# Summing the last chunk's squares on TensorE, and reading a spread norm factor from PSUM, in a two-block transformer

## The chip, the cores and the metric

The kernel runs on one core of a Trainium2 chip. A core has TensorE (matmuls; PE in the profile, with PEld for its weight loads), VectorE (DVE), ScalarE (ACT), GpSimd (POOL) and SyncE (SP), which here does nothing but issue transfers. SBUF is the working memory, PSUM the accumulators of TensorE, in eight banks of 128 partitions x 512 fp32. The metric is the device time of one execution in microseconds (us), as the median of several. TensorE's clock has two levels, 1.2 and 2.4 GHz; the profile shows the granted share of the upper one.

## The reference

Input x is 512 tokens of 1024 features, fp32, one batch. The first block is two layers of mixing and MLP, each behind an RMS norm:

```
def rms_norm(x, g):
    y = x * lax.rsqrt(jnp.mean(x * x, axis=-1, keepdims=True) + NORM_EPS)
    return y * g
for l in range(2):
    proj = rms_norm(x, mix_norm_g[l]) @ w_in[l]
    ...                     # two attentions and a gated merge
    x = x + merged @ w_out[l]
    x = x + jnp.square(jax.nn.relu(rms_norm(x, mlp_norm_g[l]) @ w_up[l])) @ w_down[l]
```

The second block works on the result h, with shifts, scales and gates made from a vector c:

```
ada = jax.nn.silu(c) @ w_ada + b_ada        # 6 x 1024 values; w_ada has 6144 columns
shift1, scale1, gate1, shift2, scale2, gate2 = jnp.split(ada, 6, axis=-1)
hn = rms_norm(h, norm1_g) * (1.0 + scale1) + shift1
h = h + gate1 * (mamba_and_sparse_attention(hn) @ w_o)
hn2 = rms_norm(h, norm2_g) * (1.0 + scale2) + shift2
h = h + gate2 * mixture_of_experts(hn2)     # 32 experts of hidden size 256, two per token
out = rms_norm(h, final_g)
```

## The kernel before

Activations lie transposed: a feature chunk is a 128x512 tile (features on the partitions, tokens along), and x is eight such chunks. A product of fp32 precision is made of three fast passes: each operand is split into hi, rounded to the fast format (`hi_pool`, line 201, on GpSimd for weights; `hi_act`, line 204, on ScalarE), and lo = x - hi (`lo_dve`, line 207, on VectorE); TensorE then does hi.hi, lo.hi and hi.lo.

**Weights** come in 128x1024 tiles of 512 KB. `Weights.load` (line 87) has SyncE load tile i into a buffer of the tag `w_st`, which has three; hi and lo go to two buffers each (`w_hi`, `w_lo`), and a tile is asked for one unit ahead of its use. A unit is what TensorE does with one tile, 24 matmuls of 128x512 in the MLP. So w_hi of tile n+2 can be written only when TensorE is through with unit n.

**The six RMS factors.** A chunk that is complete is squared by ScalarE and added to `ssq` by VectorE (`square_chunk`, line 317; `sq` is the tile of squares). When the eighth is in, `norm_factor` sums over the partitions with four pairs of narrow fp32 matmuls against a column of ones (128x2, into the PSUM tag `s1`), VectorE adds the epsilon (`r_v`, line 327) and GpSimd takes the power (`r_tm`, line 225). `norm_finish` spreads the factor: VectorE writes four diagonal tiles (line 341), TensorE multiplies them by ones into one PSUM bank of the tag `s1`, which has one buffer, and ScalarE copies that to SBUF (`r_bc`, line 344). It is done ahead of each layer's attention (24 and 756 us into the span), ahead of each MLP (405 and 1135 us), ahead of the second block (1493 us) and, through `norm_factor` alone, ahead of the experts (2427 us).

**`Block2.norm`** (1489 to 1511 us) multiplies the eight chunks by the spread factor (line 908: chunks 0, 2, 4, 6 on VectorE, 1, 3, 5 on GpSimd; line 906: chunk 7 on VectorE), adds the shift into hi on ScalarE, and makes lo on VectorE (line 910). TensorE's first unit of the second block waits for these.

**`ada_tile`** (line 875) computes the second block's shifts and gates beside the second layer's MLP, one tile of w_ada per weight unit in the 16 units before 1220 us: SyncE loads 512 KB (line 878), VectorE multiplies by silu(c) with a running sum (line 879). Its tile `wada` is of the same tag `w_st` as the weights: weight tiles and ada tiles take turns in three buffers. Weight tile n is `w_stn` in the orders below; units 166 to 181 are in this stretch.

**What sets the order.** The order of each engine's instructions, and which of a tag's buffers a tile gets, are chosen by a scheduler at build time, with a simulated timeline of the whole program. An edit in one place can so move instructions far from it.

Of the kernel before, what the change touches and what calls it, by code (L numbers as in the profile page):

```python
# [15 lines left out]
OP = mybir.AluOpType  # L16
# [3 lines left out]
P = 128  # L20
# [3 lines left out]
KC = 8  # L24
# [110 lines left out]
class K:  # L135
# [173 lines left out]
    def square_chunk(self, c, x):  # L309
        nc = self.nc  # L310
        sq = self.t([P, T], "sq", bufs=2)
        self.act(sq, x, AF.Square)
        if c == 0:
            self.ssq = self.t([P, T], "ssq")
            nc.vector.tensor_copy(self.ssq, sq)
        else:
            nc.vector.tensor_tensor(self.ssq, self.ssq, sq, op=OP.add)

    def norm_factor(self):

        nc = self.nc
        ps = self.bank("s1", 1, (P, 8))
        for tb in range(4):
            self.mm(ps[:, 2 * tb:2 * tb + 2], self.ssq[:, tb * P:(tb + 1) * P], self.ones[:, 0:2],
                    tb == 0, tb == 3, True)
        v = self.t([P, 4], "r_v")
        nc.vector.tensor_scalar(v, ps.rearrange("p (a b) -> p a b", b=2)[:, :, 0], 1.0 / D, EPS,
                                op0=OP.mult, op1=OP.add)
        r = self.t([P, 4], "r_tm", bufs=2)
        self.rsqrt(r, v)  # L330
        return r

    def norm_finish(self):

        nc = self.nc
        r = self.norm_factor()
        dg = self.t([P, T], "sq", bufs=2)
        pb = self.bank("s1", 1)
        for tb in range(4):
            c = slice(tb * P, (tb + 1) * P)  # L340
            nc.vector.tensor_scalar(dg[:, c], self.ident, r[:, tb:tb + 1], None, op0=OP.mult)
            self.mm(pb[:, c], self.ones, dg[:, c], tb == 0, tb == 3, True)
        rb = self.t([P, T], "r_bc")
        self.nc.scalar.copy(rb, pb)
        return r, rb

    def o_halves(self, dst, ps_lo, ps_hi, shape):
# [499 lines left out]
class Block2:  # L847
# [48 lines left out]
    def norm(self, x, rb, hi, lo):  # L896

        k, nc = self.k, self.k.nc
        for c in range(KC):
            s = slice(c * T, (c + 1) * T)  # L900
            shift = self.ada[:, c:c + 1]
            xc = x[c]
            if c == KC - 1:

                xc = k.t([P, T], "of", bufs=2)
                nc.vector.scalar_tensor_tensor(xc, x[c], self.mod[:, 0, c:c + 1], rb, op0=OP.mult, op1=OP.mult)
            else:
                (nc.gpsimd if c in (1, 3, 5) else nc.vector).tensor_tensor(xc, xc, rb, op=OP.mult)
            k.act(hi[:, s], xc, AF.Identity, bias=shift)
            nc.vector.scalar_tensor_tensor(lo[:, s], xc, shift, hi[:, s].bitcast(F32), op0=OP.add, op1=OP.subtract)  # L910

# [1407 lines left out]
```

## Time and profile before

| what | before |
|---|---|
| median of 3 runs | 2802.71 us (2795.55 to 2803.74) |
| profiled execution | 2804.59 us, its span 2802.5 us, granted clock 0.985 |
| TensorE (PE) busy | 2680.8 us, 96% of the span |
| VectorE (DVE) busy | 1805.6 us, 64% |
| ScalarE (ACT) busy | 982.8 us, 35% |
| GpSimd (POOL) busy | 1114.4 us, 40% |

The profile is of one execution. In a timeline a row gives the start, the time from the first start to the last end of the instructions it holds (xN), engine, line, operation, output and inputs, and in brackets how long the engine sat idle before it and what ended that. A busy TensorE is not one at its peak: at the lower clock the same matmuls take longer.

### The profile page before, as it was taken

The numbers are of one execution on the slowest core, as the hardware profiler recorded it, in microseconds if no ns is written. First come the engines' busy times: TensorE is split into PE (matmuls) and PEld (weight loads), VectorE is DVE, ScalarE is ACT, GpSimd is POOL, SyncE is SP. The second block draws the span as 40 slices with busy tenths as digits, with TensorE's granted clock in tenths as the row PEclk, the third lists the DMA queues.
The fourth block names the chain that finished last, engine by engine and source line by source line (L and its number), as shares of the span: only waits on it lengthen the run. The fifth ranks groups of instructions, "written<-read, shape, count | busy, mean of one in ns | idle before, by whom it ended". The sixth has DMA issues, their size and how long they took to land.

```text
span 2802.5 us, 36356 instructions
## 1 busy us (share of the span) xinstructions
PE 2680.8 (96%) x13308; PEld 2179.6 (78%) x13308; DVE 1805.6 (64%) x2984; ACT 982.8 (35%) x1836; POOL 1114.4 (40%) x1539
## 2 busy tenths in 40 slices
PE   7999999999989999999998999999999999799996
PEld 6788888888878878787887988776877887677774
DVE  6866553334476656555745767576777776598887
ACT  3433322011134451210212245455334233277773
POOL 4544244143264533332423445445666565201102
PEclk9999999999999999999999999999999999899998
DMA  4111232223312123456634331132212225369986
GB/s 141 53 61 47 97 120 98 98 98 107 111 62 67 38 77 134 158 180 187 193 124 148 112 118 35 53 113 78 74 64 72 68 84 199 123 239 335 357 319 229
DMA packets 112522, 355.46 MB, mean 127 GB/s; under 512 B 19559, under 2 KB 24551, under 8 KB 111696
## 3 DMA queue, kind: packets, MB, share of 16 engines
q1 hardware_dynamic: 104480, 340.61, 35.9%
q10 hardware_dynamic: 5264, 6.29, 0.6%
q0 software_dynamic: 2592, 6.15, 0.6%
q8 instruction: 107, 1.75, 0.3%
q14 instruction: 79, 0.65, 0.1%
HBM read 329.51 MB, written 27.26 MB: 127 GB/s over the span
## 4 chain that ended last, share of the span: by engine, by line
PE 75%; DVE 8%; POOL 5%; DMA 5%; issue 4%; ACT 2%; SPq 0%; POOLq 0%; DVEq 0%; ACTq 0%
PE ps_d L179 43%; PE ps_w L179 8%; PE ps_o L179 5%; PE ps_b L179 4%; PE ps_gu L179 4%; DMA wada<-in_w_ada_t 4%; PE ps_po L179 3%; PE ps_tr L179 2%; DVE w_lo L207 2%; PE ps_e L179 2%; PE ps_tr L1525 1%; PE ps_s L179 1%; POOL w_hi L201 1%; POOL W L493 1%; POOL S L1165 1%
## 5 line engine op out<-in xcount | busy, mean ns | idle before, releaser
L179 PE MATMUL ps_d<-S,w_hi 128*128 128x512 f32 x4448 | 1413.6, 395 | 20.4 <-POOL c_vec L195 7.3
L179 PEld LDWEIGHTS ps_d<-S,w_hi 128*128 128x128 f32 x4448 | 828.6, 189 | 197.8 <-POOL c_vec L195 14.5
L179 PE MATMUL ps_d<-S,w_lo 128*128 128x512 f32 x2224 | 873.3, 394 | 18.5 <-DVE w_lo L207 18.1
L201 POOL TENSOR_SCALAR w_hi<-w_st 128x1024 fp32r<-128x1024 f32 x332 | 373.6, 1125 | 731.1 <-PE ps_d L179 603.0
L207 DVE TENSOR_TENSOR w_lo<-w_st,w_hi 128x1024 fp32r<-128x1024 f32 x343 | 448.2, 1307 | 292.9 <-POOL w_hi L201 267.2
L179 PEld LDWEIGHTS ps_d<-S,w_lo 128*128 128x128 f32 x2224 | 419.2, 188 | 111.8 <-DVE w_lo L207 28.2
L217 ACT ACTIVATE f<-ps_d 128x512 f32<-128x512 f32 x64 | 38.3, 598 | 455.8 <-PE ps_d L179 455.8
L2055 POOL DMA_INDIRECT moe_rows<-my,idx x14 | 32.7, 2335 | 266.1 <-DVE my L2049 138.9
L879 DVE SCALAR_TENSOR_TENSOR W<-wada,W 128x1024 f32<-128x1024 f32 x48 | 69.6, 1449 | 97.3 <-DMA wada<-in_w_ada_t 97.3
L201 POOL TENSOR_SCALAR S<-of 128x512 fp32r<-128x512 f32 x96 | 105.3, 1097 | 67.3 <-DVE of L744 31.2
L195 POOL MEMSET c_vec<- 1x1 f32 x424 | 35.8, 89 | 238.5 <-PE ps_d L179 201.4
L1516 POOL TENSOR_SCALAR pw<-pw,ri,gn 128x128 f32<-128x128 f32 (+3 forms) x128 | 90.4, 713 | 53.9 <-DVE ri L1515 45.8
L207 DVE TENSOR_TENSOR m_lo<-S,m_hi 128x1024 fp32r<-128x1024 f32 x81 | 98.5, 1222 | 17.5 <-ACT m_hi L204 16.2
L207 DVE TENSOR_TENSOR S<-of,S 128x512 fp32r<-128x512 f32 x96 | 80.0, 833 | 33.0 <-POOL S L201 31.0
L204 ACT CAST m_hi<-S 128x1024 fp32r<-128x1024 f32 x81 | 84.5, 1049 | 29.0 <-PE ps_gu L179 13.9
L179 PE MATMUL ps_w<-w_hi,S 128*128 128x512 f32 x256 | 83.1, 403 | 9.6 <-POOL w_hi L201 9.6
L217 ACT ACTIVATE pw<-pw,mx 128x128 f32<-128x128 f32 (+3 forms) x128 | 71.4, 559 | 30.2 <-DVE mx L1513 29.5
L179 PE MATMUL ps_w<-S,w_hi 128*128 128x512 f32 x256 | 79.1, 389 | 0.0
L179 PEld LDWEIGHTS ps_tr<-gS,S 128*128 128x128 f32 x512 | 70.7, 196 | 8.7 <-issue 2.2
L179 PE MATMUL ps_tr<-gS,S 128*128 128x256 f32 x512 | 75.4, 293 | 1.1 <-DVE gS L1950 1.1
L207 DVE TENSOR_TENSOR w_lo<-S,w_hi 128x1024 fp32r<-128x1024 f32 x53 | 64.6, 1222 | 10.8 <-ACT w_hi L204 9.8
L796 DVE TENSOR_TENSOR f<-ps_d,r_sq 128x512 f32<-128x512 f32 x32 | 22.1, 690 | 73.2 <-PE ps_d L179 73.2
(576 smaller groups left out, 4815.9 us busy)
## 6 DMA issues: line engine op xcount, KB each, us to landing
w_st<-in_w SPq DMA_DIRECT2D x374, 512.0 KB, 3.3
S<-in_w SPq DMA_DIRECT2D x158, 512.0 KB, 5.6
wada<-in_w_ada_t SPq DMA_DIRECT2D x48, 512.0 KB, 3.6
x<-S SPq DMA_DIRECT2D x16, 256.0 KB, 2.0
moe_rows<-S ACTq DMA_DIRECT2D x1, 4096.0 KB, 15.7
ssm_away<-nf SPq DMA_DIRECT2D x12, 256.0 KB, 2.0
S<-in_x_t SPq DMA_DIRECT2D x8, 256.0 KB, 6.8
S<-in_x_t SPq DMA_DIRECT2D x1, 2048.0 KB, 7.6
```

The source lines that it names most:

```text
L179: return self.nc.tensor.matmul(out, l, r, start=start, stop=stop, skip_group_check=sk)
L195: b = self.nc.gpsimd.memset(self.beat_at[:, i:i + 1], 0.0)
L201: self.nc.gpsimd.tensor_scalar(hi, x, 1.0, 1.0, op0=OP.mult, op1=OP.mult)
L204: self.last_hi = self.nc.scalar.copy(hi, x)
L207: return self.nc.vector.tensor_tensor(lo, x, hi.bitcast(F32), op=OP.subtract)
L217: i = self.nc.scalar.activation(out, x, f, bias=bias, scale=scale, **kw)
L493: nc.gpsimd.tensor_scalar(p[h][:, 256 - nk:], p[h][:, 256 - nk:], ri[:, h:h + 1], 1.0, op0=OP.mult, op1=OP.mult)
L879: nc.vector.scalar_tensor_tensor(junk, w, 1.0, self.cs, op0=OP.mult, op1=OP.mult, accum_out=self.ada[:, j:j + 1])
L1165: nc.gpsimd.tensor_tensor(y, y, rb, op=OP.mult)
L1516: nc.gpsimd.tensor_scalar(w, w, ri[:, c], gate[:, c], op0=OP.mult, op1=OP.mult)
L1525: nc.tensor.transpose(pt[:, h], p[:, h, j * P:(j + 1) * P], k.ident)
L2055: self.k.nc.gpsimd.indirect_dma_start(out=self.Y, out_offset=bass.IndirectOffsetOnAxis(ap=self.idx[:, j:j + 1], axis=0), in_=y, in_offset= ...
```

## The change

`square_chunk` no longer adds the eighth chunk's squares; it keeps them in `self.sq`, and `norm_factor` sums `ssq` and `sq` with eight pairs of narrow matmuls that accumulate in the same PSUM tile, in place of four. `norm_finish` keeps its PSUM tile as `self.pb`; in `Block2.norm`, VectorE multiplies chunks 0, 1, 3, 5 and 7 by that PSUM tile, and GpSimd chunks 2, 4 and 6 by the copy in SBUF.

```diff
--- before.py
+++ after.py
@@ -313,6 +313,8 @@
         if c == 0:
             self.ssq = self.t([P, T], "ssq")
             nc.vector.tensor_copy(self.ssq, sq)
+        elif c == KC - 1:
+            self.sq = sq
         else:
             nc.vector.tensor_tensor(self.ssq, self.ssq, sq, op=OP.add)
 
@@ -320,9 +322,10 @@
 
         nc = self.nc
         ps = self.bank("s1", 1, (P, 8))
-        for tb in range(4):
-            self.mm(ps[:, 2 * tb:2 * tb + 2], self.ssq[:, tb * P:(tb + 1) * P], self.ones[:, 0:2],
-                    tb == 0, tb == 3, True)
+        for i, x in enumerate((self.ssq, self.sq)):
+            for tb in range(4):
+                self.mm(ps[:, 2 * tb:2 * tb + 2], x[:, tb * P:(tb + 1) * P], self.ones[:, 0:2],
+                        i + tb == 0, i == 1 and tb == 3, True)
         v = self.t([P, 4], "r_v")
         nc.vector.tensor_scalar(v, ps.rearrange("p (a b) -> p a b", b=2)[:, :, 0], 1.0 / D, EPS,
                                 op0=OP.mult, op1=OP.add)
@@ -342,6 +345,7 @@
             self.mm(pb[:, c], self.ones, dg[:, c], tb == 0, tb == 3, True)
         rb = self.t([P, T], "r_bc")
         self.nc.scalar.copy(rb, pb)
+        self.pb = pb
         return r, rb
 
     def o_halves(self, dst, ps_lo, ps_hi, shape):
@@ -903,9 +907,11 @@
             if c == KC - 1:
 
                 xc = k.t([P, T], "of", bufs=2)
-                nc.vector.scalar_tensor_tensor(xc, x[c], self.mod[:, 0, c:c + 1], rb, op0=OP.mult, op1=OP.mult)
+                nc.vector.scalar_tensor_tensor(xc, x[c], self.mod[:, 0, c:c + 1], k.pb, op0=OP.mult, op1=OP.mult)
+            elif c in (2, 4, 6):
+                nc.gpsimd.tensor_tensor(xc, xc, rb, op=OP.mult)
             else:
-                (nc.gpsimd if c in (1, 3, 5) else nc.vector).tensor_tensor(xc, xc, rb, op=OP.mult)
+                nc.vector.tensor_tensor(xc, xc, k.pb, op=OP.mult)
             k.act(hi[:, s], xc, AF.Identity, bias=shift)
             nc.vector.scalar_tensor_tensor(lo[:, s], xc, shift, hi[:, s].bitcast(F32), op0=OP.add, op1=OP.subtract)
 
```

VectorE has 6 instructions fewer, TensorE 24 pairs more; SyncE's order is the same. Lines from 315 on move down by 2 to 6 (line 908 becomes 912 and 914, line 879 becomes 883).

In `Block2.norm`, VectorE's rows before, from the last weight split to the first line-910 rows, with the semaphores they wait for:

```order
L207 TENSOR_TENSOR w_lo229_11621<-w_st229_11618,w_hi229_11620 128x1024 [waits DMAHW1_49,Pool_49]
L317 TENSOR_TENSOR ssq_1123_11066<-ssq_1123_11066,sq_1144_11548 128x512 [waits Activation_49]
L327 TENSOR_SCALAR r_v_1146_11556<-ps_s1_1145_11551 128x4 [waits PE_49]
L341 TENSOR_SCALAR sq_1148_11560<-c_ff_6_88,r_tm_1147_11558 128x128 [waits Pool_49]
L341 TENSOR_SCALAR sq_1148_11560<-c_ff_6_88,r_tm_1147_11558 128x128 x3
L908 TENSOR_TENSOR S2_913_8803<-S2_913_8803,r_bc_1150_11570 128x512 [waits Activation_49]
L908 TENSOR_TENSOR S2_913_8803<-S2_913_8803,r_bc_1150_11570 128x512 x3
L906 SCALAR_TENSOR_TENSOR of_1153_11595<-S2_913_8803,c_mod_1119_10996,r_bc_1150_11570 128x512 [waits DVE_49]
```

The same place with the change:

```order
L207 TENSOR_TENSOR w_lo229_11636<-w_st229_11633,w_hi229_11635 128x1024 [waits DMAHW1_49,Pool_49]
L330 TENSOR_SCALAR r_v_1146_11571<-ps_s1_1145_11562 128x4 [waits PE_49]
L344 TENSOR_SCALAR sq_1148_11575<-c_ff_6_88,r_tm_1147_11573 128x128 [waits Pool_49]
L344 TENSOR_SCALAR sq_1148_11575<-c_ff_6_88,r_tm_1147_11573 128x128 x3
L914 TENSOR_TENSOR S2_913_8812<-S2_913_8812,ps_s1_1149_11576 128x512 [waits Activation_49]
L914 TENSOR_TENSOR S2_913_8812<-S2_913_8812,ps_s1_1149_11576 128x512 x3
L910 SCALAR_TENSOR_TENSOR of_1153_11610<-S2_913_8812,c_mod_1119_11008,ps_s1_1149_11576 128x512 [waits DVE_49]
```

The last addition to ssq is gone from VectorE's row, and the first multiplication, which now reads PSUM (`ps_s1`), waits for a semaphore of ScalarE as it did before.

GpSimd's rows there before and with the change, in which only the chunks differ:

```order
L201 TENSOR_SCALAR w_hi229_11620<-w_st229_11618 128x1024 [waits DMAHW1_49,DVE_49,PE_49]
L225 TENSOR_TENSOR r_tm_1147_11558<-r_v_1146_11556,c_vec_7_90 128x4 [waits DVE_49]
L908 TENSOR_TENSOR S2_913_8803<-S2_913_8803,r_bc_1150_11570 128x512 [waits Activation_49]
L908 TENSOR_TENSOR S2_913_8803<-S2_913_8803,r_bc_1150_11570 128x512 x2
L201 TENSOR_SCALAR w_hi230_11673<-w_st230_11671 128x1024 [waits DMAHW3_49,PE_49,Pool_49]
```

```order
L201 TENSOR_SCALAR w_hi229_11635<-w_st229_11633 128x1024 [waits DMAHW1_49,DVE_49,PE_49]
L225 TENSOR_TENSOR r_tm_1147_11573<-r_v_1146_11571,c_vec_7_90 128x4 [waits DVE_49]
L912 TENSOR_TENSOR S2_913_8812<-S2_913_8812,r_bc_1150_11585 128x512 [waits Activation_49]
L912 TENSOR_TENSOR S2_913_8812<-S2_913_8812,r_bc_1150_11585 128x512 x2
L201 TENSOR_SCALAR w_hi230_11688<-w_st230_11686 128x1024 [waits DMAHW3_49,PE_49,Pool_49]
```

Its three multiplications stay, with the same wait.

In the ada stretch, VectorE's rows before, from the ada tile after weight tile 172 on:

```order
L879 SCALAR_TENSOR_TENSOR W4_912_8802,c_ada_904_8771<-wada_993_9547,W4_905_8772 128x1024
L207 TENSOR_TENSOR w_lo173_9474<-w_st173_9471,w_hi173_9473 128x1024
L207 TENSOR_TENSOR S4_945_9125<-of_984_9463,S3_942_9122 128x512
L207 TENSOR_TENSOR w_lo174_9514<-w_st174_9511,w_hi174_9513 128x1024
L879 SCALAR_TENSOR_TENSOR W4_912_8802,c_ada_904_8771<-wada_997_9587,W4_905_8772 128x1024
L207 TENSOR_TENSOR S6_946_9126<-of_988_9503,S5_943_9123 128x512
L207 TENSOR_TENSOR w_lo175_9554<-w_st175_9551,w_hi175_9553 128x1024
L879 SCALAR_TENSOR_TENSOR W4_912_8802,c_ada_904_8771<-wada_1001_9627,W4_905_8772 128x1024
L207 TENSOR_TENSOR S6_946_9126<-of_992_9543,S5_943_9123 128x512
L207 TENSOR_TENSOR w_lo176_9594<-w_st176_9591,w_hi176_9593 128x1024
L879 SCALAR_TENSOR_TENSOR W4_912_8802,c_ada_904_8771<-wada_1005_9667,W4_905_8772 128x1024
L207 TENSOR_TENSOR S6_946_9126<-of_996_9583,S5_943_9123 128x512
```

The same place with the change:

```order
L883 SCALAR_TENSOR_TENSOR W4_912_8811,c_ada_904_8780<-wada_993_9559,W4_905_8781 128x1024
L207 TENSOR_TENSOR w_lo173_9486<-w_st173_9483,w_hi173_9485 128x1024
L207 TENSOR_TENSOR S4_945_9133<-of_984_9475,S3_942_9130 128x512
L883 SCALAR_TENSOR_TENSOR W4_912_8811,c_ada_904_8780<-wada_997_9599,W4_905_8781 128x1024
L207 TENSOR_TENSOR w_lo174_9526<-w_st174_9523,w_hi174_9525 128x1024
L207 TENSOR_TENSOR S6_946_9134<-of_988_9515,S5_943_9131 128x512
L883 SCALAR_TENSOR_TENSOR W4_912_8811,c_ada_904_8780<-wada_1001_9639,W4_905_8781 128x1024
L207 TENSOR_TENSOR w_lo175_9566<-w_st175_9563,w_hi175_9565 128x1024
L207 TENSOR_TENSOR S6_946_9134<-of_992_9555,S5_943_9131 128x512
L883 SCALAR_TENSOR_TENSOR W4_912_8811,c_ada_904_8780<-wada_1005_9679,W4_905_8781 128x1024
L207 TENSOR_TENSOR w_lo176_9606<-w_st176_9603,w_hi176_9605 128x1024
L207 TENSOR_TENSOR S6_946_9134<-of_996_9595,S5_943_9131 128x512
```

Before, w_lo174 stands ahead of the ada tile wada_997, and so it goes on. With the change w_lo174 to w_lo178 stand behind the ada tile that precedes them. The buffers move too: with the change each of wada_973, 977, 981 and so on to 1013 (eleven tiles) is loaded into the buffer of the weight tile whose w_lo stands just ahead of it in VectorE's order (wada_973 in that of w_st167, wada_1013 in that of w_st177); before, that holds for five tiles, wada_981 to wada_997. w_lo166 and w_lo167 are parted too: with the change the ada tile wada_969 stands between them.

## Rows read from the trace of the kernel before

**Rows 1.** Windows: busy us of each engine, granted clock, DMA share, GB/s.
```profile
400.00:420.00 20.00, 20.00 (x98) 16.81 (x97) 8.67 (x13) 5.52 (x9) 9.86 (x9) 1.00 0.25 81
740.00:770.00 30.00, 30.00 (x148) 25.36 (x147) 10.65 (x13) 1.73 (x3) 7.50 (x8) 1.00 0.30 97
1489.40:1512.60 23.20, 13.38 (x47) 9.21 (x47) 16.36 (x26) 7.20 (x11) 8.26 (x6) 0.71 0.50 190
2500.00:2750.00 250.00, 243.85 (x1180) 186.11 (x1179) 214.27 (x323) 177.66 (x284) 32.69 (x14) 0.99 0.93 337
```

**Rows 2.** Timeline of 1489 to 1499 us, up to the spread factor.
```profile
1491.15 0.63 ACT L217 ACTIVATE sq<-S 128x512 f32<-128x512 f32 x1 [8.06 <-DVE S L797]
1492.18 0.68 DVE L317 TENSOR_TENSOR ssq<-ssq,sq 128x512 f32<-128x512 f32 x1
1493.00 1.02 PE L179 MATMUL ps_s<-c_ff,ssq 128*128 128x2 f32 x8 [3.55 <-DVE ssq L317]
1497.89 0.59 ACT L344 COPY r_bc<-ps_s 128x512 f32<-128x512 f32 x1 [6.11 <-PE ps_s L179]
```

**Rows 3.** Timeline of 1499 to 1516 us, the multiplications and behind.
```profile
1498.51 5.74 DVE L908 TENSOR_TENSOR S<-S,r_bc 128x512 f32<-128x512 f32 x4 [2.26 <-ACT r_bc L344]
1498.55 5.14 POOL L908 TENSOR_TENSOR S<-S,r_bc 128x512 f32<-128x512 f32 x3 [3.21 <-ACT r_bc L344]
1500.10 0.76 PE L179 MATMUL ps_b<-S,w_hi 128*128 128x512 f32 x1 [2.25 <-ACT S L217]
...
1504.83 4.05 DVE L910 SCALAR_TENSOR_TENSOR S<-S,c_ada,S 128x512 fp32r<-128x512 f32 x6
1510.26 0.98 PE L179 MATMUL ps_b<-S,w_hi 128*128 128x512 f32 x3 [0.53 <-DVE S L910]
```

**Rows 4.** Instructions of line 908: ns min/median/max.
```profile
L908 DVE TENSOR_TENSOR S<-S,r_bc x4: 693/1759/1765, 1498.5 to 1502.5; 128x512 f32<-128x512 f32 x4
```

**Rows 5.** Instructions of line 678, which multiply a PSUM tile.
```profile
L678 DVE TENSOR_TENSOR S<-ps_d,r_bc x16: 677/692/694, 98.6 to 978.2; 128x512 f32<-128x512 f32 x16
```

**Rows 6.** GpSimd's groups by shape: busy us, mean ns, idle before.
```profile
L1496 POOL TENSOR_TENSOR S<-nsa_c,rk 128x512 f32<-128x512 f32 x2 | 2.1, 1043 | 2.0 <-DVE rk L1491 2.0
```

**Rows 7.** Timeline at 405 us, the MLP norm's sums amid matmuls.
```profile
405.32 0.39 PE L179 MATMUL ps_d<-S,w_hi 128*128 128x512 f32 x1
406.36 0.49 PE L179 MATMUL ps_d<-S,w_hi 128*128 128x512 f32 x1
```

**Rows 8.** Timeline at 1139 us, the second MLP's first weights.
```profile
1139.27 0.80 PE L179 MATMUL ps_d<-S,w_lo 128*128 128x512 f32 x1 [2.80 <-DVE w_lo L207]
```

**Rows 9.** Timeline at 26 us.
```profile
26.74 0.79 PE L179 MATMUL ps_w<-w_lo,S 128*128 128x512 f32 x1 [1.52 <-DVE w_lo L207]
```

**Rows 10.** Timeline at 2426 us.
```profile
2426.23 0.66 PE L1717 MATMUL ps_e<-c_ff,S 128*128 128x128 f32 x4 [0.62 <-DVE S L1709]
```

**Rows 11.** Timeline of 1154 to 1163 us: one round of the ada stretch.
```profile
1155.61 1.21 DVE L207 TENSOR_TENSOR w_lo<-w_st,w_hi 128x1024 fp32r<-128x1024 f32 x1
1156.86 0.33 SPq L878 DMA_DIRECT2D wada<-in_w_ada_t  x1
1161.31 1.23 DVE L879 SCALAR_TENSOR_TENSOR W<-wada,W 128x1024 f32<-128x1024 f32 x1 [3.88 <-DMA wada<-in_w_ada_t]
```

**Rows 12.** VectorE's timeline of 1129 to 1225 us.
```profile
1143.10 1.23 DVE L879 SCALAR_TENSOR_TENSOR W<-wada,W 128x1024 f32<-128x1024 f32 x1 [0.28 <-DMA wada<-in_w_ada_t]
1181.46 1.23 DVE L879 SCALAR_TENSOR_TENSOR W<-wada,W 128x1024 f32<-128x1024 f32 x1 [2.86 <-DMA wada<-in_w_ada_t]
```

**Rows 13.** GpSimd's timeline of 1136 to 1220 us.
```profile
1211.26 1.06 POOL L201 TENSOR_SCALAR w_hi<-w_st 128x1024 fp32r<-128x1024 f32 x1 [2.64 <-PE ps_d L179]
...
1216.70 1.06 POOL L201 TENSOR_SCALAR w_hi<-w_st 128x1024 fp32r<-128x1024 f32 x1 [2.64 <-PE ps_d L179]
```

**Rows 14.** Timeline of 2771 to 2776 us, the last experts.
```profile
2771.82 3.37 DVE L2154 TENSOR_TENSOR S<-S,my 128x1024 f32<-128x1024 f32 x1
2775.39 1.22 PE L179 MATMUL ps_po<-m_hi,mhs 128*128 128x512 f32 x2 [4.26 <-DVE mhs L207]
```

## The prediction

> **What bounds the kernel now.** I read the busy shares first: TensorE is at work for 96% of the span (the table). So I went by windows, to see where it isn't. In the layers it is busy for all of a stretch (20.00 of 20 us, 30.00 of 30); around the second block's norm it is busy for 13.38 of 23.2 us, at a mean granted clock of 0.71; among the experts it is at 244 of 250 us while the transfers take 0.93 of the DMA engines [rows 1]. Time saved on another engine counts only where TensorE waits for it. Then I read the timelines of the six norms and, with the order of instructions beside them, of the stretches in which instructions moved.
>
> **Second block's norm (the part that both edits meet).** The eighth chunk's squares are ready at 1491.15 + 0.63 = 1491.78; the addition (0.68) follows, and TensorE starts its sums at 1493.00 [rows 2]. With the change the sum of `ssq` can be done before, and that of `sq` starts some 0.1 us behind ScalarE, at 1491.9: 1.1 us gained, with four pairs behind it as before. All that follows up to the copy, which ends at 1497.89 + 0.59 = 1498.48 [rows 2], comes 1.1 sooner, at 1497.4. VectorE's multiplications don't start before that copy ends: their first instruction waits for ScalarE in the order with the change. Reading PSUM therefore doesn't take the copy off the path; without that wait they would start 0.6 us sooner.
>
> The Trainium skill (PSUM — Partial Sum Buffer, section "PSUM bank collisions raise a hardware error") says that two engines must not touch the same bank and quadrant at one time, two readers included, and that the back end therefore adds a dependency between them. By that rule the wait is forced, as ScalarE's copy and VectorE's multiplication read one bank; the order with the change agrees, and no run so far shows what it costs. By the rule the sum stays as it is worked out below; were readers free of one another, it would be 0.6 us less.
>
> What reading PSUM can change is how long the multiplications take. Before, VectorE's four take 5.74 us while GpSimd's three take 5.14 [rows 3], and one of the four took 693 ns while the median is 1759 [rows 4]: the two engines take turns. Multiplications that read one operand from PSUM take 692 ns in 16 cases [rows 5], and GpSimd, with the same shape from SBUF, 1043 ns on average [rows 6]. I take 0.69 and 1.04, since the rows before show VectorE slow only in the company of GpSimd with both operands in SBUF; at the other end they stay at 1.76. VectorE then needs 4 x 0.69, 0.69 for chunk 7 and 8 x 0.675 for the lo's (4.05 for six [rows 3]), in all 8.9 us: its last lo is done at 1506.3, and TensorE, which ends 1.0 us behind its last wait for a lo [rows 3], at 1507.3. By TensorE itself: its unit is 24 matmuls, which take 5.44 us at the upper clock (5.44 us from unit to unit among the layers [rows 13], 0.227 each) and twice that, 10.9, at the lower, which is half of it; from a first hi 1.1 us sooner than 1500.10 [rows 3] it would end at 1509.9 if the clock never rose. The clock of 0.71 in the stretch says that it does rise on the way. Before, the unit ended at 1510.26 + 0.98 = 1511.24. Between 1507.3 and 1509.9 I take 1508.6: **-2.6 us**; the ends are -1.1 (the multiplications stay slow) and -4.0.
>
> **The sums in the middle of matmuls.** Four pairs of narrow sums at 405 us part two matmuls by 406.36 - 405.32 = 1.04 us [rows 7], where they would be 0.23 apart: 0.81 us. TensorE is full there and at 756 us [rows 1], so four pairs more cost 2 x 0.81 = **+1.6 us** (0 to 2.9, the upper end for pairs that are strewn among matmuls). VectorE's additions that go were hidden there: nothing comes back. At 1135 us TensorE waits 2.80 us for VectorE's w_lo right behind [rows 8], and the extra pairs go into that wait: 0, and 0.81 without it. At 26 us TensorE waits 1.52 us for a w_lo [rows 9] that stands behind the last addition on VectorE: **-1.0** (-1.5 to 0). At 2426 us the pairs partly fill a wait of 0.62 [rows 10]: **+0.4** (0 to 1).
>
> **The ada stretch (1135 to 1220 us), a side effect.** Here the order moves. Before, five ada tiles are loaded into the buffer of the weight tile whose w_lo stands just ahead of them on VectorE. Each round is a ring that nothing overlaps: w_lo at 1155.61 to 1156.8, issue at 1156.86, multiplication at 1161.31 when the tile is in [rows 11], and then the next w_lo. From the multiplication at 1161.31 three rounds lead to that at 1181.46: 6.72 us each [rows 11, 12]. TensorE needs 1216.70 - 1211.26 = 5.44 us for a unit [rows 13]. So such a round holds it back by 1.28 us when no lead is left. After five, w_lo174 stands ahead of the ada tile and the ring is broken.
>
> With the change there are eleven rounds in a row. The multiplication of wada_969, at 1143.10 [rows 12] in both orders, ends at 1144.3, w_lo167 behind it at 1145.4, and w_lo178 eleven rounds of 6.72 later, at 1219.3. Unit 178 needs it from its second matmul on, so it ends near 1219.3 + 23 x 0.227 = 1224.5. Before, unit 178 ended at 1216.70, when its buffer went to w_hi of tile 180 [rows 13]. The difference is **+7.8 us**; nothing behind gives it back, since TensorE bounds the units that follow. The ends are 0 (the ring isn't the limit, or transfers land sooner) and +11 (rounds of 7). SyncE's order is the same, and behind each waiting ada issue on its queue stands the next weight load, which is 2 rounds ahead of its use.
>
> **Experts and tail.** Many rows of the experts are interleaved anew, with equal work. In the tail an addition of line 2154 (3.37 us) stands on VectorE just ahead of the lo on which TensorE waits 4.26 us [rows 14]; with the change it stands five rows sooner, but GpSimd's four additions, which slow VectorE there, end when they did. I take **0** (-4 to +5).
>
> **Sum.** -2.6 + 1.6 - 1.0 + 0.4 + 7.8 + 0 = +6.2 us on the profiled execution of 2804.59. That one is 1.9 above the median of 2802.71; the forecast for the median is 2802.71 + 6.2 = 2808.9, say 2809, 0.22% slower.
>
> **Rivals.**
> - *The ring does not hold TensorE back.* The five rounds before cost less than 5 x 1.28 in all if a lead was there, and a transfer may land sooner. Then the rest is left: 6.2 - 7.8 = -1.6, 2801. Against it: eleven rounds use up any lead that five did not.
> - *The experts are worse interleaved.* There the DMA engines are at 0.93 [rows 1], and one weight tile is 512 KB; at 337 GB/s that is 1.6 us by itself. Where a weight load's issue moves behind a use, one load is bare; with three or more such places beyond the ring, 5 us come on top: 2814. For it: the rows there are shuffled widely. Against it: SyncE's order, by which the loads go out, is the same. It decides from a third such place on.
> - *The kernel gets faster.* The norm gains its 4.0, the sums hide altogether, the ring costs nothing and the experts gain 4: -4.0 - 1.5 - 4 = -9.5 with the gain of 1.5 at 26 us, 2793. It needs all of these at once; the wait on ScalarE's copy already takes a part of what the edit could give.
> - *The change does not do what it says*: VectorE reads PSUM but stays at 1.76 us a multiplication. Only 1.1 of the 2.6 is left and the sum is +7.7: 2810. This lies in the forecast's own range.
>
> **How the numbers follow.** What a measurement of this kernel can tell from no change is about 0.3%, 8.4 us: below 2794.3 is faster, above 2811.1 slower. The forecast with its own range of 2805 to 2815 has 0.61 (0.38 of it within the bound, 0.23 above), no ring 0.15 (within), worse experts 0.16 (above), faster 0.08 (0.07 below the bound). That makes 0.07 faster, 0.54 the same, 0.39 slower. The range of 2800 to 2818 leaves out the faster case, a part of no ring and the top of worse experts.
>
> **What would show it.** In the profile after: TensorE's sums of `sq` at 0.1 us behind ScalarE's last square and the first unit of the second block done 2 to 4 us sooner after the layers' end; VectorE's multiplications at 0.69 us, the first right behind ScalarE's copy; between 1150 and 1220 us, ada multiplications 6.7 us apart eleven times, TensorE idle for 1.3 us in each, and the unit of tile 178 done 8 us later than the start of the stretch would give. The prediction is wrong if those multiplications come 5.4 apart, or if the stretch of the experts differs by more than 4 us.

## The result, and the profile after

The change makes the kernel slower: 2816.29 us as the median of five runs (2815.54 to 2822.29) against 2800.08 us before (2795.55 to 2803.74, the three runs shown and two more), a ratio of 1.0058 with a 95% interval of 1.0047 to 1.0069. That is 16.2 us more. The direction was forecast, and the time lies in the stated range of 2800 to 2818, but above the forecast's own part of it (2805 to 2815): 6.2 us were forecast, 16.2 came. The profiled execution after took 2817.3 us (span 2815.5), 12.7 more than the one before, which was among the slower ones of its kernel.

Where the time went is read best from marks that both traces have: ScalarE's squares, of which the last of a norm follows the unit that completes x, and its copy behind the second block's first unit. The table gives the time from each mark's start to the next. Three of the marks in ScalarE's timeline before:

```profile
1125.72 0.62 ACT L217 ACTIVATE sq<-S 128x512 f32<-128x512 f32 x1
...
1415.00 0.64 ACT L217 ACTIVATE sq<-S 128x512 f32<-128x512 f32 x1 [11.29 <-DVE S L797]
...
1511.27 0.59 ACT L927 COPY pT<-ps_b 128x512 f32<-128x512 f32 x1 [5.00 <-PE ps_b L179]
```

and such rows after:

```profile
398.39 0.62 ACT L217 ACTIVATE sq<-S 128x512 f32<-128x512 f32 x1
...
750.27 0.62 ACT L217 ACTIVATE sq<-S 128x512 f32<-128x512 f32 x1
...
1130.36 0.62 ACT L217 ACTIVATE sq<-S 128x512 f32<-128x512 f32 x1
...
1431.65 0.63 ACT L217 ACTIVATE sq<-S 128x512 f32<-128x512 f32 x1 [11.29 <-DVE S L801]
...
1523.99 0.58 ACT L933 COPY pT<-ps_b 128x512 f32<-128x512 f32 x1 [4.06 <-PE ps_b L179]
```

| stretch, from mark to mark | before | after | difference |
|---|---|---|---|
| start to the last square at the first MLP norm | 396.28 | 398.39 | +2.1 |
| to the last square at the second attention norm | 350.97 | 351.88 | +0.9 |
| to the last square at the second MLP norm | 378.47 | 380.09 | +1.6 |
| to the first square at the second block's norm (the ada stretch and what follows) | 289.28 | 301.29 | **+12.0** |
| to the last square there | 76.15 | 76.16 | 0.0 |
| to the copy behind the first unit of the second block | 20.12 | 16.18 | **-3.9** |
| to the last square ahead of the experts | 914.94 | 914.60 | -0.3 |
| to `r_v` ahead of the experts | 2.50 | 3.36 | +0.9 |
| to the end | 373.76 | 373.55 | -0.2 |

The tiles of w_ada don't end at 1220 us: of the 48 that VectorE multiplies, 32 follow, up to 1397 us before and 1415 after, and the fourth stretch holds these too. The sum is +13.0, the difference of the spans. The first stretch is no effect to build on: in the eleven further profiles below it takes 395.0 to 400.4 us.

**The second block's norm** gained more than forecast. The timeline after, around it [rows 2, 3]:

```profile
1507.81 0.63 ACT L217 ACTIVATE sq<-S 128x512 f32<-128x512 f32 x1 [8.06 <-DVE S L801]
1508.49 1.22 PE L179 MATMUL ps_s<-c_ff,sq 128*128 128x2 f32 x8 [1.60 <-ACT sq L217]
...
1513.56 0.58 ACT L347 COPY r_bc<-ps_s 128x512 f32<-128x512 f32 x1 [5.13 <-PE ps_s L179]
1514.18 2.48 DVE L914 TENSOR_TENSOR S<-S,ps_s 128x512 f32<-128x512 f32 x4 [2.26 <-ACT r_bc L347]
1514.22 3.76 POOL L912 TENSOR_TENSOR S<-S,r_bc 128x512 f32<-128x512 f32 x3 [3.21 <-ACT r_bc L347]
...
1517.23 4.61 DVE L916 SCALAR_TENSOR_TENSOR S<-S,c_ada,S 128x512 fp32r<-128x512 f32 x6
...
1523.22 0.73 PE L179 MATMUL ps_b<-S,w_hi 128*128 128x512 f32 x2 [0.27 <-DVE S L916]
```

The sums start 0.05 us behind ScalarE's square. VectorE starts its multiplications 0.62 us behind the start of ScalarE's copy, with that copy as what ended its wait, as the order had said. Its four take 2.48 us in place of 5.74, and GpSimd's three 3.76 in place of 5.14.

**The ada stretch** lost more than forecast. VectorE's multiplications of ada tiles after, the first and the last of twelve [rows 11, 12]:

```profile
1146.24 1.23 DVE L883 SCALAR_TENSOR_TENSOR W<-wada,W 128x1024 f32<-128x1024 f32 x1 [2.84 <-DMA wada<-in_w_ada_t]
...
1221.26 1.23 DVE L883 SCALAR_TENSOR_TENSOR W<-wada,W 128x1024 f32<-128x1024 f32 x1 [3.12 <-DMA wada<-in_w_ada_t]
```

Eleven rounds in 75.02 us, 6.82 each: the ring is there, about as long as forecast (6.72). What the forecast lacked shows in TensorE's windows after (busy us, granted clock, DMA share, GB/s):

```profile
1160.00:1170.00 10.00, 7.05 (x30) 1.00 0.39 128
1170.00:1175.00 5.00, 4.85 (x14) 0.66 0.49 163
1175.00:1225.00 50.00, 42.98 (x182) 1.00 0.47 156
1225.00:1230.00 5.00, 5.00 (x17) 0.66 0.71 217
```

The clock falls to its lower level for a while, in the ring, at its end, and once more in the stretch behind it (0.69 from 1265 to 1270 us). A mean of 0.66 over 5 us is 1.7 us lost. The kernel before has one such fall in the stretch, behind its wait of 2.80 us [rows 8]:

```profile
1139.00:1143.00 4.00, 3.73 (x10) 0.57 0.80 252
```

With the change that wait isn't there. Ahead of each fall after stands one of TensorE's longest waits for a low half. The first, in TensorE's timeline after:

```profile
1162.36 0.50 PE L179 MATMUL ps_d<-S,w_lo 128*128 128x512 f32 x1 [1.07 <-DVE w_lo L207]
...
1163.16 0.40 PE L179 MATMUL ps_d<-S,w_lo 128*128 128x512 f32 x1
...
1170.15 0.50 PE L179 MATMUL ps_d<-S,w_lo 128*128 128x512 f32 x1 [2.03 <-DVE w_lo L207]
...
1171.95 0.63 PE L179 MATMUL ps_d<-S,w_lo 128*128 128x512 f32 x1
1172.38 1.05 PE L179 MATMUL ps_d<-S,w_hi 128*128 128x512 f32 x2
1173.23 0.63 PE L179 MATMUL ps_d<-S,w_lo 128*128 128x512 f32 x1
```

Behind the wait of 1.07 us the matmuls keep about their pace: the low-half matmuls, which stand three matmuls apart, are 0.80 us apart (1162.36 to 1163.16). Soon behind that of 2.03 us they are 1.28 us apart (1171.95 to 1173.23), 0.43 for one matmul. This wait is longer because the split took longer. In the timeline of all engines:

```profile
1161.15 2.07 POOL L201 TENSOR_SCALAR w_hi<-w_st 128x1024 fp32r<-128x1024 f32 x1 [3.13 <-PE ps_d L179]
...
1167.98 1.04 POOL L201 TENSOR_SCALAR w_hi<-w_st 128x1024 fp32r<-128x1024 f32 x1 [3.74 <-PE ps_d L179]
1168.00 0.08 DVE L883 DVE_READ_ACCUMULATOR W<-wada,W 128x1 f32 x1
1168.00 2.10 DVE L207 TENSOR_TENSOR w_lo<-w_st,w_hi 128x1024 fp32r<-128x1024 f32 x1
...
1170.12 0.33 SPq L882 DMA_DIRECT2D wada<-in_w_ada_t  x1
1173.88 1.22 DVE L883 SCALAR_TENSOR_TENSOR W<-wada,W 128x1024 f32<-128x1024 f32 x1 [2.77 <-DMA wada<-in_w_ada_t]
```

The low half of the next tile, which takes 1.21 us by itself [rows 11], begins 0.02 us behind GpSimd's high half of another and is done only 1.1 us behind its end. The ada tile's issue comes behind that, at 1170.12: this is the ring. In the round before, VectorE's low half began first, at 1161.09, 0.06 us ahead: it took 1.22 us, and GpSimd's high half 2.07. So it is in all the profiles here, from 1100 to 1480 us, wherever two such splits begin within 0.3 us of each other: the later one is drawn out, by 0.7 to 1.1 us. A few hundredths of a us decide whether that is the low half, for which TensorE waits.

Unit 178, the last that the ring holds back, ends where GpSimd starts the high half of tile 180 [rows 13]; GpSimd's timeline after:

```profile
1231.73 1.06 POOL L201 TENSOR_SCALAR w_hi<-w_st 128x1024 fp32r<-128x1024 f32 x1 [6.79 <-PE ps_d L179]
```

**The sums amid matmuls** stand apart in TensorE's row; the second four pairs at 409 us, in the timeline after:

```profile
408.57 0.95 PE L179 MATMUL ps_s<-c_ff,sq 128*128 128x2 f32 x8
```

The stretch from 398 to 750 us, which holds them, is 0.9 us longer in every kernel with that term (351.88 us against 350.97 or 350.98 in all others).

### The profile page after: what moved, and what is told of

Same layout as the page of the kernel before. It is cut to its first block, busy times and chain, and to the rows that moved or that the text cites. A ratio compares the mean times of both kernels' runs of the same rounds, so it can differ in the third digit from the quotient of the medians.

```text
span 2815.5 us, 36446 instructions
## 1 busy us (share of the span) xinstructions
PE 2688.9 (96%) x13356; PEld 2188.7 (78%) x13356; DVE 1799.8 (64%) x2978; ACT 981.8 (35%) x1836; POOL 1114.1 (40%) x1539
## 4 chain that ended last, share of the span: by engine, by line
PE 74%; DVE 8%; DMA 5%; POOL 5%; issue 4%; ACT 3%; SPq 0%; DVEq 0%; POOLq 0%; ACTq 0%
PE ps_d L179 43%; PE ps_w L179 8%; DMA wada<-in_w_ada_t 4%; PE ps_o L179 4%; PE ps_b L179 4%; PE ps_gu L179 4%; PE ps_po L179 3%; DVE w_lo L207 2%; PE ps_tr L179 2%; PE ps_e L179 2%; PE ps_tr L1531 1%; PE ps_s L179 1%; POOL w_hi L201 1%; POOL W L497 1%; POOL S L1171 1%
## 5 line engine op out<-in xcount | busy, mean ns | idle before, releaser
L201 POOL TENSOR_SCALAR S<-f 128x512 fp32r<-128x512 f32 x56 | 54.5, 974 | 36.7 <-ACT f L216 32.1
```

Of the source, the lines that this page charges most:

```text
L201: self.nc.gpsimd.tensor_scalar(hi, x, 1.0, 1.0, op0=OP.mult, op1=OP.mult)
```

## The experiments

Theory A: most of the time is the ring of ada tiles, which the second term at the second MLP's norm alone brings about. Theory B: the second terms cost 2 to 3 us at each norm, and the ring takes up slack only. All ratios are against the kernel before on the same chip, with 95% intervals; its median was 2800.02 us beside runs 1 to 4, 2805.41 beside 5 to 8 and 2802.07 beside 9 to 11.

**1. The sums alone.** `Block2.norm` reads `r_bc` throughout and divides the chunks as before.

```diff
...
-                nc.vector.tensor_tensor(xc, xc, k.pb, op=OP.mult)
+                (nc.gpsimd if c in (1, 3, 5) else nc.vector).tensor_tensor(xc, xc, rb, op=OP.mult)
```

> Only the sums are changed, at all six norms; the second block's multiplications read the copy in SBUF, split as before. Theory A (most of the 16 us comes from the ring of the ada tiles, which the sums at the second MLP's norm bring about): the ring is there, so about 16 us plus what reading PSUM gains, 2818 us (2814 to 2822). Theory B (the extra pairs of sums and the waits around them cost 2 to 3 us at every norm, and the ring only takes up slack): the same time, 2816 to 2820. The run tells what the second edit is worth: A and my forecast say 1.5 to 3 us less gain than the full change at the second block's norm.

Measured: 2811.42 us, ratio 1.0049 (1.0035 to 1.0062). Below what either theory gave (at least 2814), though the ring is there. The ada stretch took 296.19 us in its profile (before 289.28). The stretch at the second block's norm took 18.97, so the sums are worth 1.15 us of the gain there, and the second edit the other 2.8. Its profile is that of its fastest run, 2806.75, and shows one fall of the clock in the ring where the change shows two and a third behind it; the two falls that it lacks go with units of 9.4 and 9.7 us, where it has 6.9 and 7.8: most of the 5 us by which the two stretches differ (301.29 and 296.19). The runs go up to 2817.83, at a mean granted clock of 0.984 against 0.988 in the fastest: the clock varies from run to run of one kernel, though only the profiles show where, and the gain of 2.8 us lies within that spread. Unit 178 ends 98.5 us behind the mark at the second MLP norm (1124.87 us here) in place of 101.4, as GpSimd's timeline of this run shows:

```profile
1223.32 1.05 POOL L201 TENSOR_SCALAR w_hi<-w_st 128x1024 fp32r<-128x1024 f32 x1 [3.76 <-PE ps_d L179]
```

**2. The PSUM reads alone.** The sums are as before.

```diff
-        elif c == KC - 1:
-            self.sq = sq
...
-        for i, x in enumerate((self.ssq, self.sq)):
-            for tb in range(4):
...
+        for tb in range(4):
...
```

> Only the second block's norm is changed: VectorE reads the factor from PSUM for chunks 0, 1, 3, 5, 7 and GpSimd takes 2, 4, 6; all squares are summed as before. Theories A and B: no ring, no extra pairs; the multiplications take 0.69 us in place of 1.76, the first unit of the second block ends 1.5 to 3 us sooner, and the time is 2797 to 2799. A third view, that the wait for ScalarE's copy eats the gain: 2800, no change, with VectorE's multiplications still near 1.7 us.

Measured: 2800.86 us, 0.9998 (0.9988 to 1.0007). The stretch at the norm took 18.19 us in place of 20.12, the multiplications 682 ns on average; a gain of 1.9 us in the trace that the runs, with their spread of 9 us, don't show in the total. The forecast of 2797 to 2799 for the total was missed.

**3. All but the second MLP's norm.** There the eighth chunk's squares are added by VectorE again; five norms keep the second term.

```diff
-        elif c == KC - 1:
+        elif c == KC - 1 and self.norm_no() in (0, 1, 2, 4, 5):
             self.sq = sq
```

> The full change, but ahead of the second layer's MLP the eighth chunk's squares are added by VectorE as before (five norms of six keep the second term). Theory A: no ring, so 2816 less 12 to 14: 2800 to 2804, with ada multiplications as before (5.2 to 6.7 us apart). Theory B: only one of six norms is taken back: 2812 to 2815.

Measured: 2803.69 us, 1.0010 (1.0001 to 1.0020). The ada stretch takes 288.84 us, as before. Theory B is out.

**4. The second MLP's norm alone.** The kernel before with the second term there and nowhere else (`in (3,)`), with `Block2.norm` as before.

> The kernel before with one thing changed: ahead of the second layer's MLP, and only there, the eighth chunk's squares are a second term on TensorE. Theory A: eleven rounds of the ring, 6.7 to 6.9 us apart, and 10 to 14 us more: 2810 to 2814. Theory B: one norm costs 2 to 3 us: 2802 to 2803.

Measured: 2819.14 us, 1.0071 (1.0057 to 1.0085): 19 us for one norm's four pairs of sums and one addition less, more than theory A gave. The ada stretch took 300.10 us (+10.8) with rounds of 6.6 to 7.9 us, and the stretch of the experts 378.8 us (+5.0). The latter stays open: the same stretch takes 369 to 379 us over the kernels here, whose order of rows differs there.

**5. The full change, with the order mended.** Each ada tile's multiplication is held behind the low half that was split last when the tile is asked for. With it the buffers go otherwise too: an ada tile takes that of a weight tile whose low half stands two places ahead of its multiplication (the rows under run 6), so the run tests order and buffers together.

```diff
-            k.split(hi, lo, st, act=self.act)
+            self.last_lo = k.split(hi, lo, st, act=self.act)
...
-        nc.vector.scalar_tensor_tensor(junk, w, 1.0, self.cs, op0=OP.mult, op1=OP.mult,
-                                       accum_out=self.ada[:, j:j + 1])
+        i = nc.vector.scalar_tensor_tensor(junk, w, 1.0, self.cs, op0=OP.mult, op1=OP.mult,
+                                           accum_out=self.ada[:, j:j + 1])
+        k.tc.add_manual_dep(i.ins, k.W.last_lo.ins.name, SYNC, reason="order")
```

> The full change with one thing added: each ada tile's multiplication is held behind the low half of the weight tile that was split last when the tile was asked for, so that on VectorE no weight split of the next two units stands behind a waiting ada tile. All sums and PSUM reads stay. Theory A (the ring costs the time): the multiplications come one unit apart (5.44 us), TensorE's waits between 1150 and 1335 us go (15.5 us of them in the profile of the change) and with them the dips of the clock; 2800 us (2796 to 2804). Theory B (the sums and where they stand cost it): 2812 to 2817.

Measured: 2791.58 us, 0.9954 (0.9937 to 0.9970). Faster than the kernel before and than the 2796 to 2804 expected, with all six second terms in place: theory A holds, and the waits in this stretch had cost more than the difference of the two kernels.

**6. The kernel before, with the same order.**

> The kernel before, with the same order added. Theory A: its five rounds cost something as well: TensorE waits 9.4 us for low halves between 1130 and 1335 us there, of which about 4 to 6 go: 2794 to 2797. Theory B: no change, 2800.

Measured: 2787.32 us, 0.9942 (0.9927 to 0.9956): 16 us of the 2800 were the five rounds, the other waits for low halves that the kernel before has up to 1335 us, and what followed them, where 4 to 6 had been expected. The ada stretch takes 274.12 us in place of 289.28. In this order the change (run 5) is 4 us slower than the kernel before, with intervals that overlap, in place of 16: by itself, without the ring, it gains nothing in the total. The windows of 1130 to 1335 us (busy us of TensorE first, then its weight loads and the other engines, clock, DMA share, GB/s), before:

```profile
1130.00:1335.00 205.00, 195.47 (x848) 157.72 (x847) 120.80 (x145) 23.96 (x39) 65.95 (x55) 0.99 0.56 177
```

with the change:

```profile
1130.00:1335.00 205.00, 189.26 (x803) 150.49 (x802) 112.84 (x134) 21.21 (x35) 61.92 (x51) 0.98 0.51 163
```

and the kernel before in the mended order:

```profile
1130.00:1335.00 205.00, 205.00 (x914) 170.00 (x913) 124.04 (x157) 27.66 (x45) 73.53 (x61) 1.00 0.60 191
```

TensorE is never idle there, its clock never falls, and it gets through 914 matmuls in the time in which the change gets through 803. VectorE's rows in that kernel show why:

```profile
1152.77 1.23 DVE L207 TENSOR_TENSOR w_lo<-w_st,w_hi 128x1024 fp32r<-128x1024 f32 x1 [1.86 <-POOL w_hi L201]
1155.11 1.22 DVE L879 SCALAR_TENSOR_TENSOR W<-wada,W 128x1024 f32<-128x1024 f32 x1
1156.26 0.08 DVE L879 DVE_READ_ACCUMULATOR W<-wada,W 128x1 f32 x1
1158.21 1.23 DVE L207 TENSOR_TENSOR w_lo<-w_st,w_hi 128x1024 fp32r<-128x1024 f32 x1 [1.87 <-POOL w_hi L201]
...
1166.00 1.22 DVE L879 SCALAR_TENSOR_TENSOR W<-wada,W 128x1024 f32<-128x1024 f32 x1
```

and the issue that follows the second low half, in the timeline of all engines:

```profile
1159.46 0.33 SPq L878 DMA_DIRECT2D wada<-in_w_ada_t  x1
```

The ada tile is there when VectorE comes to it (no wait ahead of it), and low halves come 5.44 us apart. The buffer that the low half of 1158.21 frees takes the ada tile that is multiplied at 1166.00, behind one more low half: the transfer has a whole unit's time.

**7. The mended order, with the second term at two norms** (the first attention's and the second block's), and the PSUM reads.

> The ordered kernel with the second term kept only at the first layer's attention norm and at the second block's norm, where TensorE waits for VectorE's addition, and with the PSUM reads. Theory A: against the ordered kernel before, 3.9 us less at the second block's norm and up to 1 at the start: 2789 to 2794, faster than both kernels. Theory B: 2797 to 2800.

Measured: 2787.72 us, 0.9943 (0.9930 to 0.9957), faster than the kernel before and the change, but no faster than run 6. The stretch at the second block's norm is 17.25 us against 20.93 there, so 3.7 us were gained; the stretch of the experts took 377.1 against 372.0.

**8. The second operand from SBUF, with the chunks divided as in the change** (`rb` for `k.pb`).

> The full change, but VectorE reads the copy in SBUF as its second operand; chunks stay divided as in the change (2, 4, 6 on GpSimd). If the place of the operand makes the difference: VectorE's multiplications stay near 1.76 us, and from the last squares to the copy behind the first unit it takes about 19 us (18.97 us in the run with the sums alone) in place of 16.2. If the division of the chunks makes it: multiplications at 0.69 us and 16.2 us. The ring stays: total about 2815 to 2820.

Measured, one execution: 2815.24 us. VectorE's and GpSimd's groups there (busy us, mean ns, idle before):

```profile
L914 DVE TENSOR_TENSOR S<-S,r_bc 128x512 f32<-128x512 f32 x4 | 5.7, 1492 | 2.3 <-ACT r_bc L347 2.3
L912 POOL TENSOR_TENSOR S<-S,r_bc 128x512 f32<-128x512 f32 x3 | 5.1, 1741 | 3.2 <-ACT r_bc L347 3.2
```

and with the change:

```profile
L914 DVE TENSOR_TENSOR S<-S,ps_s 128x512 f32<-128x512 f32 x4 | 2.5, 682 | 2.3 <-ACT r_bc L347 2.3
L912 POOL TENSOR_TENSOR S<-S,r_bc 128x512 f32<-128x512 f32 x3 | 3.8, 1275 | 3.2 <-ACT r_bc L347 3.2
```

The stretch took 18.74 us. It is the place of the operand that makes VectorE and GpSimd faster side by side, not the division of the chunks.

**9 to 11. What is worth keeping.** In the mended order: the PSUM reads alone; these with the second term at the second block's norm only; and the same with all eight chunks on VectorE and no copy for them. The second of these differs from run 7 by one line:

```diff
-        elif c == KC - 1 and self.norm_no() in (0, 4):
+        elif c == KC - 1 and self.norm_no() in (4,):
```

> The ordered kernel before with the PSUM reads of the second block's norm alone (VectorE 0, 1, 3, 5, 7 from PSUM, GpSimd 2, 4, 6); sums as before. Last squares to the copy behind the first unit: about 18 us (18.19 in the run with this edit alone) in place of 20.9. Total 2 to 3 us under the ordered kernel before, which had 0.9942 of the kernel before: ratio about 0.993.

> The ordered kernel with the PSUM reads, and the second term of the sums at the second block's norm only. The stretch takes 16.2 to 16.5 us (3.9 less than before); elsewhere no sum is longer. If a gain in that stretch reaches the end of the kernel, the ratio is about 0.9928; if the later stretches give it back, 0.994.

> As the last one, but all eight chunks are multiplied by VectorE from PSUM, and ScalarE makes no copy for the second block, so that VectorE's first multiplication waits for TensorE alone. It starts 0.6 us sooner against ScalarE's last squares. VectorE then has 8 x 0.66 + 8 x 0.675 = 10.7 us of work in place of 8.9, so the last low half is about 1.2 us later; TensorE, at the lower clock, is the bound or not: the stretch takes 16 to 17.5 us, the ratio is that of the last one within 0.001.

Measured: 2788.97 us, 0.9949 (0.9935 to 0.9963); 2783.82 us, **0.9927** (0.9910 to 0.9945); 2786.20 us, 0.9937 (0.9923 to 0.9952). The stretch at the norm took 18.13, 17.22 and 16.36 us; for run 10, 16.2 to 16.5 had been expected. Run 10 has the lowest ratio of all, with its whole interval below 1 and below that of the change; among the four kernels of the mended order with little else (6, 7, 9, 10) the intervals overlap, so that what the norm's edits add is seen in their stretch and not in the total. Run 10's stretch is longer than that because TensorE's clock rose late, with the 14th matmul of the unit (1490.43 us, 14.4 us behind the start of the last square) where the change has it with the eighth (1519.22, 11.4 us behind). VectorE's last low half was done at 1491.8, and TensorE, not VectorE, ended the unit, at 1493.2. In run 11, without ScalarE's copy, VectorE starts 0.03 us behind the matmuls that spread the factor, in place of 0.65 with the change; but it then has all eight chunks, 10.2 us of work in place of 9.0, and the stretch is no shorter than the 16.18 us that the change took with the copy.

## Why the prediction was right in its direction and short in its size

- **The ring** (+7.8 forecast): found as forecast, with its place, its eleven rounds and their length (6.82 us against 6.72), and shown as the cause by runs 3, 4 and 5. Its size was the step that failed: +12.0 in the profiled stretch, and the change is 12 to 13 us slower by medians than the kernel of run 3, which lacks it. The forecast priced TensorE at the upper clock and the last low half at 1.1 us. Up to the end of unit 178, where GpSimd starts the high half of tile 180, it was 91.0 us from the mark at the second MLP norm before (1216.70 [rows 13] - 1125.72) and 101.4 with the change (1231.73 - 1130.36): +10.4. Against the forecast's +7.8, the ring began 1.5 us sooner, its rounds were 1.1 longer in all, the last low half took 2.05 us (+0.9), and unit 178, from the end of its wait at 1224.52, 7.2 in place of 5.2 (+2.0), since the clock fell in it. In run 1, where the low half took 1.22 us and the clock did not fall there, the same end came 98.5 us behind the mark (1223.32 - 1124.87): +7.5. The other 1.6 of the 12.0 stand behind the ring, where the third fall is. The first fall, amid the rounds, cost the ring little: the ada multiplication behind it came 7.04 us after the one before, and the two units that followed had no wait.
- The same +12.0 by kind: 6.2 are TensorE's idle time (9.5 us before, 15.7 after, by the windows under run 6), 3.4 the lower clock (three falls against one, 1.7 each), 0.9 the sums at this norm (275.03 us in run 5 against 274.12 in run 6); 1.5 are not assigned. That the falls come from the waits is read from their order in time; no run changed one without the other.
- **The second block's norm** (-2.6 forecast): -3.9, at the end of its range. The sums' part was right to a tenth (1.15 in run 1 against 1.1), as was the wait on ScalarE's copy; the multiplications at 0.68 us freed 2.8 us and not 1.5. The forecast's middle between VectorE's bound and TensorE's was too far to TensorE's for this execution: its clock rose at 1519.2 us, with the eighth matmul of 24, and VectorE's work was the bound, 9.0 us (1514.18 to 1523.16) where 8.9 were forecast. In runs 7 and 10 the clock rose later, TensorE was the bound, and the stretches, 17.25 and 17.22 us, lie 2.9 under the kernel before.
- **The sums amid matmuls** (+1.6): 0.91 us at 405 us where 0.81 was forecast; at 756 us the stretch grew by 1.6 but differs by 4 to 5 us among kernels with the same sums, so it can't be told. At 1135 us they were to go into the wait of 2.80 us, at no cost; that wait is gone with the change, and the 0.9 us are paid. The 1.0 us at 26 us wasn't seen in the marks either, since the start differs by more. At 2426 us it is +0.9 for a forecast of 0.4.
- **The experts and the tail** (0): -0.2 here, but 369 to 379 us over all the kernels. The bounds were fair, the zero was luck. The rival with worse experts had 2814 us, nearest to what was measured, but its cause isn't there.
- **No ring** as a rival assumed that five rounds had cost little. Run 6 shows the opposite: they, the waits around and behind them and the fall of the clock cost the kernel before 15 us, of which 9.5 are TensorE's idle time in the window to 1335 us.

## What to carry to other kernels

When two kinds of tile take turns in one set of buffers, follow each engine's order for the instruction that frees a buffer and the one that waits for the refill: if both stand in one row, the transfer's whole latency is in the loop, whatever prefetch depth the code asks for. An edit that moves one small instruction can make such a ring longer at a place it never touches, and the edit's own cost is then beside the point; hold the order by a dependency before judging the edit. In a stretch at full TensorE load, waits can cost more than their sum, where the granted clock falls behind them (here 3.4 us on top of 6.2).

## What the runs showed of the hardware

- TensorE's clock fell to the lower level behind single waits of 2.03, 2.03 and 2.54 us in the profile of the change, of 2.11, 2.25 and 2.12 in that of run 4, of 2.09 in that of run 1 and of 2.80 in the kernel before (granted 0.57 to 0.69 over 4 or 5 us, which is 1.7 us lost each), with an otherwise nearly full row before. Behind two others, 2.06 in run 4 and 2.03 in run 1, it did not, nor behind any of 0.8 to 1.1 us. The profiles of runs 2, 3 and 8 hold six more waits of 2.03 to 2.81 us in this stretch, each with a fall.
- A low half on VectorE and a high half on GpSimd (128x1024) that overlap: the one that begins first takes its 1.22 or 1.04 us, the other up to 2.1; a lead of 0.02 to 0.06 us was enough (1167.98 and 1168.00, 1161.09 and 1161.15 us with the change).
- VectorE's multiplication of two SBUF operands and GpSimd's side by side take 1492 and 1741 ns on average; with one of VectorE's operands in PSUM 682 and 1275.
- Two readers of one PSUM bank were kept one behind the other: VectorE began 0.62 us behind the start of ScalarE's copy of 0.58 us, and 0.03 us behind TensorE where there was no copy (run 11).
